# Three of eight second feed-forward products by seven half-size products, and another search for the order

## The chip, the core and the metric

The kernel runs on one core of a Trainium2 chip. The metric is the device time of one execution in microseconds; a kernel's time is the median of its executions. TensorE multiplies, VectorE (DVE) and ScalarE (ACT) work element by element, GpSimd (POOL) does little here, and SyncE (SP) issues the DMAs that bring weights from HBM.

## What is computed

Two layers act on 512 rows of 1024 numbers. Each mixes the rows (a pooling mixer and a sparse attention, from one input projection) and then runs a feed-forward. All is in float32:

```python
for l in range(DEPTH):                       # DEPTH = 2, D_FF = 4096
    h = rms_norm(x, g_pre_mix[l])
    proj = h @ w_in[l]
    ...
    mix = jnp.concatenate([a_out, b_out], axis=-1) @ w_out[l]
    x = x + rms_norm(mix, g_post_mix[l])
    h = rms_norm(x, g_pre_ffn[l])
    f = jnp.square(jax.nn.relu(h @ w_ff1[l])) @ w_ff2[l]
    x = x + rms_norm(f, g_post_ffn[l])
```

The change lies in the line of `f`.

## The kernel before

**Precision.** A float32 number is held as a high half and a low half (value minus high half), both in a format that TensorE takes at full rate. A product is three matmuls (`PASSES`, L823: high by high, high by low, low by high). So every operand of TensorE costs one copy (high half; VectorE or ScalarE, whichever the planner picks, `copy`, L656) and one subtraction (low half; VectorE alone, `tt`, L648).

**Weights.** `WeightStream` (L418) takes all weights in one fixed sequence. Raw tiles come by DMA: two tiles `wraw` for plain loads, two tiles `uraw` (ring `t8`) for units. Each chunk of 128 rows by 512 columns is split into one of eight tiles `ws` (`NWS`, L36), and the next is split when TensorE has used one up (`done`, L581). A unit (`add_unit`, L461) is the weights of one product by sevens: two raw tiles, from which `_combine` (L539) makes fourteen tiles: seven combinations of quarters, each in two parts. Four sums per raw tile (all VectorE) are made in place at the combination S2; a raw tile is given back after its last combination, 22.

**The feed-forward** (L1107 to L1245). The 4096 hidden units are eight blocks of 512. Block 0's first product is plain. For blocks 1 to 7 `unit_products` (L1132) computes the first product of a block as seven products of half size (Winograd's form of Strassen's scheme): 168 matmuls of 256 columns. Three partial results are kept (`kept`), the four quarters are added up, passed through relu and square, and split into `f` (`evac`). Two blocks make a group (`g`, L1184): after both first products comes the group's second product, plain: for each half of the 1024 columns, eight chunks by four row tiles by three passes, into four banks. These are then copied to (first group) or added to (`facc`, VectorE) the sum of the layer, 8 instructions of 512 columns per group.

**Banks.** Eight PSUM banks: a ring of four (`pg`: second product and `unit_products`), a ring of two (`pm`: transposes), two single ones (`pq`). The feed-forward uses the last four only in block 0.

**The order.** The program does not run as written: `Planner` (L83) records each operation with its dependences, the engines it may run on and a cost, and `issue` (L193) searches for an order. A sweep schedules all operations by a key, a second one backward gives each its latest time, and that becomes the next key. `SWEEPS` (L98) is 40, from one beginning; the order with the shortest planned span is issued, each engine's instructions in that order. TensorE's instructions of neighbouring products are mixed where the plan says so. All instructions carry line 372, where the recorder calls the engine, so the rows are read by tiles.

Of the kernel before, what the change touches and what calls it, by code (L numbers as in the profile page):

```python
# [16 lines left out]
OP = mybir.AluOpType  # L17
# [18 lines left out]
NWS = 8  # L36
NRAW = 2
# [45 lines left out]
class Planner:  # L83
# [9 lines left out]
    DMA_LANDS = 1050  # L93
    CELL = 64
# [3 lines left out]
    SWEEPS = 40  # L98
# [89 lines left out]
    def lag(self, ea, eb):  # L188
        if eb == "sp":
            return self.DMA_STARTS  # L190
        return self.DMA_LANDS if ea == "sp" else self.LATENCY.get((ea, eb), 150)

    def issue(self):  # L193

        ops = self.ops
        n = len(ops)
        succ = [[] for _ in range(n)]
        pred = [[] for _ in range(n)]  # L200
        for i, (_, deps, soft) in enumerate(ops):
            for group, hard in ((deps, True), (soft, False)):
                for d in group:
# [9 lines left out]
        state, key, late, best = self.SEED, [], None, None  # L213
        for r in rank:
            state = (state * 1103515245 + 12345) % 2 ** 31
            key.append(self.NOISE * (state / 2.0 ** 31 - 0.5) - r)
        for _ in range(self.SWEEPS):
            start, end, way = self.sweep(key, pred, succ, late)
            span = max(end)
            if best is None or span < best[0]:  # L220
                best = (span, start, way)
            back, _, _ = self.sweep([-t for t in end], succ, pred, None, way)
            late = [span - b for b in back]
            key = [late[i] - ops[i][0][way[i]][1] for i in range(n)]
        self.planned, start, way = best
        for i in sorted(range(n), key=lambda i: (start[i], i)):
            ops[i][0][way[i]][2]()
# [131 lines left out]
class _Recorder:  # L359
# [3 lines left out]
    def __getattr__(self, method):  # L363
        def call(*args, **kw):
# [4 lines left out]
            reads = [a for k, a in list(enumerate(args))[1:] + list(kw.items())  # L369
# [19 lines left out]
    def cost(self, method, args, kw, out, reads):  # L389
# [20 lines left out]
        if self.name == "pool":  # L410
            if method == "memset":
                return 50
            return (70 + 1.2 * n) if method == "tensor_scalar" else (520 if n == 1 else 50 + 2.35 * n)
        nbytes = math.prod(c for _, c in out.ap) * 4
# [3 lines left out]
class WeightStream:  # L418
# [5 lines left out]

    COMBINATIONS = ("11", "12", "S2", "S1", "S3", "S4", "22")

    def __init__(self, copy, tt, sp, raw_pool, ws_pool, unit_pool, sum_pool):
        self.copy, self.tt, self.sp = copy, tt, sp
# [32 lines left out]
    def add_unit(self, src, r0, c0):  # L461

        k = len(self.loads)
        for cp in range(2):
            self.loads.append((src, r0 + 2 * cp * P, "unit", c0, 512))
# [16 lines left out]
    def _ahead(self):  # L482

        while self.n_load < len(self.loads):
            unit = self.loads[self.n_load][2] == "unit"
# [5 lines left out]
    def _load(self):  # L491
# [3 lines left out]
        if n == "unit":  # L495
# [5 lines left out]
            for k in range(2):  # L501
                self.sp.dma_start(t[:, k], src[r + 4 * k * P:r + (4 * k + 2) * P, c0:c0 + ncols].rearrange(
# [36 lines left out]
    def _combine(self, k, name, w):  # L539
# [3 lines left out]

        def quarter(i, j):
            return raw[:, j, :, 256 * i:256 * i + 256]

        def v(ap):
            return ap.rearrange("p (c n) -> p c n", c=2)
# [3 lines left out]
        def halves(value):  # L552
            self.copy(high, value)
            self.tt(low, value, high.bitcast(F32), OP.subtract)
# [31 lines left out]
def hymba_trunk(ctx: ExitStack, tc: tile.TileContext, x, positions, g_pre_mix, w_in, w_pool,  # L586
# [4 lines left out]
        ("pe", nc.tensor), ("act", nc.scalar), ("dve", nc.vector), ("pool", nc.gpsimd), ("sp", nc.sync))]  # L591
    ctx.enter_context(tc.manual_schedule())
# [72 lines left out]
    ws = WeightStream(copy, tt, sp, rawp, wsp, t8p, sup)  # L665
    plan = []
    for l in range(DEPTH):
# [14 lines left out]
        for g in range(4):  # L682
            for b in (2 * g, 2 * g + 1):
                p["ff1", b] = ws.add_unit(w_ff1[l], 0, 512 * b) if b else ws.add(w_ff1[l], 0, D, 512 * b, 512)
            for hf in range(2):
                p["ff2", g, hf] = ws.add(w_ff2[l], 1024 * g, 1024, 512 * hf, 512)
# [183 lines left out]
    for l in range(DEPTH):  # L870
# [261 lines left out]
        def unit_products(ids, f):  # L1132
# [21 lines left out]
            def evac(rows, cols, value, other=None):  # L1154
                r = t2("fr")[:, :512]
                if other is not None:
                    dve.tensor_tensor(r, value, other, op=OP.add)
                    value = r
                planner.either(lambda: act.activation(r, value, AF.Relu),
                               lambda: dve.tensor_scalar(r, value, 0.0, None, op0=OP.max))  # L1160
                squared(r, r)
                rv = r.rearrange("p (j n) -> p j n", j=2)
                hi = f[0][:, 2 * rows:2 * rows + 2, cols]
                copy(hi, rv)
                tt(f[1][:, 2 * rows:2 * rows + 2, cols], rv, hi.bitcast(F32), OP.subtract)
# [4 lines left out]
            evac(0, LATER, two, p1)  # L1170
# [6 lines left out]
            evac(1, SOONER, one, p5)  # L1177
            product(two, "S4", "22")
            evac(0, SOONER, two, u2)
            product(one, "22", "T4")  # L1180
            evac(1, LATER, one)

        facc = None
        for g in range(4):  # L1184
            f1 = []
            for bi in range(2):
                blk = 2 * g + bi
                if bi == 0:
                    f = [c2a.tile([P, 4, S], F32R, name="f1h", tag="c2a"), c2b.tile([P, 4, S], F32R, name="f1l", tag="c2b")]
                else:  # L1190
                    f = c1p.tile([P, 2, 4, S], F32R, name="f1", tag="c1")
                    f = [f[:, 0], f[:, 1]]
                f1.append(f)
                ids = p["ff1", blk]

                def evac_f(j, ps, cols):
                    r = t2("fr")[:, :ps.shape[1]]
                    planner.either(lambda: act.activation(r, ps, AF.Relu),
                                   lambda: dve.tensor_scalar(r, ps, 0.0, None, op0=OP.max))
                    squared(r, r)  # L1200
                    copy(f[0][:, j, cols], r)
                    tt(f[1][:, j, cols], r, f[0][:, j, cols].bitcast(F32), OP.subtract)

                if blk == 0:
                    for tp in (1, 0):
                        cols = slice(256 * tp, 256 * tp + 256)
                        for j in range(4):
                            bank = pq(j, "pf")[:, :256]
                            for kc in range(KC):
                                w = ws.get(ids[kc])  # L1210
                                mm3(bank, lambda a: w[:, a, j * P:(j + 1) * P],
                                    lambda b: A[:, b, kc, cols], kc == 0, kc == KC - 1)
                                if tp == 0 and j == 3:
                                    ws.done()
                            evac_f(j, bank, cols)
                else:
                    unit_products(ids, f)
            if facc is None:
                facc = c0p.tile([P, NT, D], F32, name="facc", tag="c0")
            for hf in range(2):  # L1220
                ids = p["ff2", g, hf]
                cs = slice(512 * hf, 512 * hf + 512)
                banks = [pg() for _ in range(NT)]
                last = g == 3 and hf == 1

                def step(c, t):
                    w = ws.get(ids[c])
                    f = f1[c // 4]
                    mm3(banks[t], lambda a: f[a][:, c % 4, tok(t)], lambda b: w[:, b, :512], c == 0, c == KC - 1)

                for c in range(4 if last else KC):
                    for t in range(NT):
                        step(c, t)
                    ws.done()
                if last:
                    for t in range(NT):
                        for c in range(4, KC):
                            step(c, t)
                            if t == NT - 1:
                                ws.done()  # L1240
                for t in range(NT):
                    if g == 0:
                        copy(facc[:, t, cs], banks[t])
                    else:
                        dve.tensor_tensor(facc[:, t, cs], banks[t], facc[:, t, cs], op=OP.add)  # L1245
        ws.units_allowed = False
# [31 lines left out]
```

## Time and profile before

| | |
|---|---|
| median of three executions | 1188.26 us (1187.7 to 1189.58) |
| the profiled execution | 1189.19 us, span 1187.4 us |
| TensorE busy | 1154.9 us, 97% |
| VectorE busy | 962.8 us, 81% |
| ScalarE busy | 593.5 us, 50% |
| DMA | 115.55 MB, mean 97 GB/s |
| matmuls | 6888 |

The table is of one execution, from its first instruction to its last. Busy time is the time in which at least one instruction of the engine runs; matmuls are pipelined, so a busy TensorE is not yet one at its peak, and its pace has to be read from starts. A stage is judged by itself, since the feed-forward and the attention have different limits.

### The profile page before, as it was taken

What the parts mean: (1) busy time and instruction counts of PE and PEld (TensorE: products, weight loads), DVE (VectorE), ACT (ScalarE), POOL (GpSimd) and SP (SyncE); (2) the same over time, 40 slices, a digit from 0 to 9 for tenths busy, and PEclk for the clock granted to TensorE, in tenths of its full rate; (3) what the DMA queues carried; (4) which work ended last, traced back from release to release, by engine and by line L of the source; (5) the groups of instructions that cost most, each with busy time, mean ns of one, the idle gap of its engine ahead of it and who ended that gap; (6) DMA issues with size and microseconds to landing.
All of it is one profiled execution on the core that took longest, in us unless ns stands there. A gap on an engine that the chain in (4) does not pass through costs nothing.

```text
span 1187.4 us, 18436 instructions
## 1 busy us (share of the span) xinstructions
PE 1154.9 (97%) x6888; PEld 1008.9 (85%) x6888; DVE 962.8 (81%) x2134; ACT 593.5 (50%) x1279; POOL 31.5 (3%) x79
## 2 busy tenths in 40 slices
PE   6999999999999999999999999899999999999997
PEld 6988888789899898899898888777998998988985
DVE  7799999889569579577698999998994785875965
ACT  7545796687226036035275277876760440430621
POOL 2000000010000000000010000001000000000001
PEclk9999998999999999999999999999999999999999
DMA  7221222451423223223233121134542241251231
GB/s 249 71 72 36 71 72 72 142 184 66 161 74 132 95 72 132 82 71 97 60 112 89 54 72 54 54 115 134 160 141 73 71 161 54 72 177 36 72 107 71
DMA packets 62169, 115.55 MB, mean 97 GB/s; under 512 B 5248, under 2 KB 10368, under 8 KB 62080
## 3 DMA queue, kind: packets, MB, share of 16 engines
q1 hardware_dynamic: 62080, 114.38, 30.2%
q8 instruction: 54, 0.88, 0.3%
q14 instruction: 35, 0.29, 0.1%
HBM read 112.27 MB, written 2.10 MB: 96 GB/s over the span
## 4 chain that ended last, share of the span: by engine, by line
PE 61%; DVE 26%; DMA 5%; ACT 4%; issue 3%; POOL 1%; SPq 0%; DVEq 0%; ACTq 0%; POOLq 0%
PE pg L372 33%; PE one L372 9%; PE two L372 7%; DVE ws L372 6%; DVE bias L372 3%; PE pi L372 3%; PE pf L372 3%; DVE m L372 3%; DMA wraw<-in_w_out_dram 2%; DMA uraw<-in_w_ff_dram 2%; DVE mx L372 1%; PE lg L372 1%; DVE s L372 1%; PE po L372 1%; DVE pT L372 1%
## 5 line engine op out<-in xcount | busy, mean ns | idle before, releaser
L372 PE MATMUL pg<-ws,f 128*128 128x512 f32 x768 | 230.5, 394 | 0.0
L372 PE MATMUL pg<-ws,A 128*128 128x512 f32 x864 | 227.5, 401 | 0.9 <-DVE A L372 0.6
L372 ACT ACTIVATE ws<-wraw 128x512 fp32r<-128x512 f32 (+1 forms) x182 | 112.9, 632 | 183.8 <-PE pg L372 127.3
L372 DVE TENSOR_TENSOR ws<-wraw,ws 128x512 fp32r<-128x512 f32 (+1 forms) x288 | 194.4, 689 | 5.9 <-ACT ws L372 3.8
L372 PEld LDWEIGHTS pg<-ws,A 128*128 128x128 f32 x864 | 157.7, 188 | 34.3 <-DVE pn L372 1.6
L372 PE MATMUL pg<-ws,f1h 128*128 128x512 f32 x512 | 167.2, 394 | 0.5 <-ACT fr L372 0.5
L372 PEld LDWEIGHTS pg<-ws,f 128*128 128x128 f32 x768 | 141.1, 188 | 29.0
L372 PEld LDWEIGHTS pg<-ws,f1h 128*128 128x128 f32 x512 | 95.6, 188 | 22.3 <-ACT fr L372 1.0
L372 DVE TENSOR_TENSOR ws<-uraw,ws 128x512 fp32r<-128x512 f32 x168 | 111.7, 686 | 2.0 <-ACT ws L372 0.7
L372 DVE CAST ws<-wraw 128x512 fp32r<-128x512 f32 (+1 forms) x106 | 45.0, 426 | 75.2 <-PE pg L372 64.3
L372 PE MATMUL two<-A,ws 128*128 128x256 f32 x672 | 104.9, 281 | 0.0
L372 PE MATMUL pg<-ws,f1l 128*128 128x512 f32 x256 | 95.8, 393 | 0.0
L372 PEld LDWEIGHTS two<-A,ws 128*128 128x128 f32 x672 | 92.3, 188 | 1.9
L372 ACT ACTIVATE ws<-uraw 128x512 fp32r<-128x512 f32 x95 | 57.7, 627 | 67.8 <-PE pg L372 29.7
L372 ACT ACTIVATE s<-s,st 128x384 f32<-128x384 f32 (+3 forms) x118 | 64.7, 565 | 21.4 <-DVE st L372 20.8
L372 ACT ACTIVATE fr<-fr 128x512 f32<-128x512 f32 (+1 forms) x109 | 63.5, 596 | 21.0 <-DVE fr L372 20.1
L372 DVE TENSOR_TENSOR facc<-pg,facc 128x512 f32<-128x512 f32 x48 | 32.7, 688 | 46.2 <-PE pg L372 46.2
L372 DVE CAST ws<-uraw 128x512 fp32r<-128x512 f32 x73 | 30.4, 424 | 41.7 <-PE pg L372 32.6
L372 PE MATMUL pi<-ws,A 128*128 128x292 f32 x384 | 61.8, 310 | 1.1 <-DVE ws L372 0.8
L372 PE MATMUL pool<-A,ws 128*128 128x512 f32 x192 | 59.2, 405 | 0.0
L372 PEld LDWEIGHTS pg<-ws,f1l 128*128 128x128 f32 x256 | 48.0, 188 | 10.9
L372 PE MATMUL one<-A,ws 128*128 128x256 f32 x336 | 57.0, 280 | 0.0
(189 smaller groups left out, 2203.5 us busy)
## 6 DMA issues: line engine op xcount, KB each, us to landing
wraw<-in_w_ff_dram SPq DMA_DIRECT2D x72, 512.0 KB, 3.8
uraw<-in_w_ff_dram SPq DMA_DIRECT2D x56, 512.0 KB, 4.9
wraw<-in_w_out_dram SPq DMA_DIRECT2D x32, 512.0 KB, 3.7
wraw<-in_w_in_dram SPq DMA_DIRECT2D x24, 512.0 KB, 3.6
wraw<-in_w_in_dram SPq DMA_DIRECT2D x8, 584.0 KB, 4.3
wraw<-in_w_in_dram SPq DMA_DIRECT2D x16, 256.0 KB, 2.9
x<-in_x_dram SPq DMA_DIRECT2D x4, 512.0 KB, 6.5
out_dram<-x SPq DMA_DIRECT2D x8, 256.0 KB, 2.1
```

The lines of the kernel that those rows point to most:

```text
L372: lambda: getattr(self.real, method)(*args, **kw), self.port(method, out, reads))
```

## The change

In blocks 1, 3 and 5 of each layer the second product too is made of seven half-size products; blocks 0, 2, 4, 6 and 7 keep the plain one (`PLAIN_FF2`). The product is now made block by block, not group by group, and block b's second product stands after the first product of block b + 1. The hidden values of a block whose second product goes by sevens are split into seven operands (three quarters and four combinations, with four subtractions) instead of four quarters. The seven products go into two pairs of banks from `pm` and `pq`, and what stands in a pair after each product is added to `facc`, 14 adds per block. The loads of two gains move from the start of the feed-forward to block 6, since the hidden values use their buffers. The search starts from twelve beginnings with 16 sweeps each; all but the first start near the best order so far. A path that would let DMAs do the subtractions is in the code, with nothing selected (`SUMMED_BY_DMA` is empty).

```diff
+PLAIN_FF2 = (0, 2, 4, 6, 7)
...
-    SWEEPS = 40
+    SWEEPS = 16
+    BEGINNINGS = 12
...
+        for begin in range(self.BEGINNINGS):
+            key, late = [], None
+            for i in range(n):
+                state = (state * 1103515245 + 12345) % 2 ** 31
+                mine = -rank[i] if begin == 0 else best[1][i] + best[3][i]
+                key.append(self.NOISE * (1 + 3 * (begin > 0)) * (state / 2.0 ** 31 - 0.5) + mine)
+            for _ in range(self.SWEEPS):
...
+    SUMMED_BY_DMA = {"unit": (), "wide": ()}
...
+    def add_unit(self, src, r0, c0, wide=False):
...
+            if wide:
+                self.loads.append((src, r0 + cp * P, "wide", c0, 1024))
...
+        ff1(0)
+        ff2(0)
+        ff1(1)
+        for b in range(1, 8):
+            if b < 7:
+                ff1(b + 1)
+            ff2(b)
...
-        load_gain(("post_ffn", l), g_post_ffn, l)
-        if l + 1 < DEPTH:
-            load_gain(("pre_mix", l + 1), g_pre_mix, l + 1)
...
+                unit_products(p["ff1", b], put, room)
+                U["T1"] = place(3)
+                U["T2"] = [A[:, a, 0:2, SOONER] for a in range(2)]
+                U["T3"] = [A[:, a, 2:4, SOONER] for a in range(2)]
+                tt(r["11"], r["12"], r["11"], OP.subtract)
+                split(U["T1"], r["11"])
+                tt(r["12"], r["22"], r["12"], OP.subtract)
+                tt(r["22"], r["22"], r["11"], OP.subtract)
+                tt(r["21"], r["21"], r["22"], OP.subtract)
...
+        def ff2_unit(b, U):
+            ids = p["ff2", b]
+            def product(banks, name, other, new, *quarter):
+                for c in range(2):
+                    w = ws.get(ids[name][c])
+                    for t in range(2):
+                        for i, (a, b) in enumerate(PASSES):
+                            pe.matmul(banks[t], U[other][a][:, c, P * t:P * t + P], w[:, b, :512],
+                                      start=new and c == i == 0, stop=c == 1 and i == 2, skip_group_check=True)
+                    ws.done()
+                cs = slice(512 * quarter[0], 512 * quarter[0] + 512)
+                for t in range(2):
+                    acc = facc[:, (2, 0)[quarter[1]] + t, cs]
+                    dve.tensor_tensor(acc, banks[t], acc, op=OP.add)
+            one = [pm("one2"), pm("one2")]
+            two = [pq(i, "two2") for i in range(2)]
+            product(one, "11", "11", True, 0, 0)
+            product(two, "12", "21", True, 0, 0)
+            product(one, "S2", "T2", False, 0, 1)
+            two = [pq(i, "two2") for i in range(2)]
+            product(two, "S1", "T1", True, 1, 1)
+            product(one, "S3", "T3", False, 1, 1)
+            product(two, "S4", "22", False, 0, 1)
+            product(one, "22", "T4", False, 1, 0)
+        f = {0: ff1_block(0)}
+        ff2_plain(0, f.pop(0))
+        f[1] = ff1_block(1)
+        for b in range(1, 8):
+            if b < 7:
+                f[b + 1] = ff1_block(b + 1)
+            if b == 6:
+                load_gain(("post_ffn", l), g_post_ffn, l)
+                if l + 1 < DEPTH:
+                    load_gain(("pre_mix", l + 1), g_pre_mix, l + 1)
+            if b in PLAIN_FF2:
+                ff2_plain(b, f.pop(b))
+            else:
+                ff2_unit(b, f.pop(b))
```

## Rows read from the trace of the kernel before

**Rows 1.** The page's head: span, busy time and share of each engine.
```profile
span 1187.4 us, 18436 instructions
PE 1154.9 (97%) x6888; PEld 1008.9 (85%) x6888; DVE 962.8 (81%) x2134; ACT 593.5 (50%) x1279; POOL 31.5 (3%) x79
```

**Rows 2.** Table by stretch, feed-forward groups: length, busy (instructions), clock, DMA, GB/s.
```profile
core 0: us, PE busy (x) PEld busy (x) DVE busy (x) ACT busy (x) POOL busy (x), PEclk, DMA share, GB/s
381.55:470.55 89.00, 87.69 (x541) 77.96 (x541) 64.32 (x112) 29.44 (x53) 0.00 (x0) 1.00 0.32 106
470.55:552.67 82.12, 81.61 (x516) 73.55 (x517) 59.37 (x104) 27.89 (x48) 0.11 (x1) 1.00 0.25 81
297.17:552.67 255.50, 253.27 (x1583) 226.92 (x1583) 182.72 (x318) 89.09 (x155) 0.11 (x1) 1.00 0.30 100
880.57:1134.47 253.90, 253.37 (x1584) 227.35 (x1584) 182.00 (x319) 85.31 (x149) 0.00 (x0) 1.00 0.30 98
```

**Rows 3.** Chain of waits, in order of time, 280 to 340 us: start, us, what.
```profile
291.03 2.85 PE two L372 x24
293.88 2.70 PE one L372 x23
...
297.17 37.12 PE pg L372 x160
```

**Rows 4.** The page's groups of instructions: the second product's matmuls.
```profile
L372 PE MATMUL pg<-ws,f 128*128 128x512 f32 x768 | 230.5, 394 | 0.0
...
L372 PE MATMUL pg<-ws,f1h 128*128 128x512 f32 x512 | 167.2, 394 | 0.5 <-ACT fr L372 0.5
...
L372 PE MATMUL pg<-ws,f1l 128*128 128x512 f32 x256 | 95.8, 393 | 0.0
```

**Rows 5.** VectorE's longest wait in 276:582 and in 858:1172: total, times, longest.
```profile
DVE ws L372 <- PE pg L372: 50.5, 30, 5.3
DVE ws L372 <- PE pg L372: 46.4, 31, 4.9
```

**Rows 6.** Table by stretch again, columns as in rows 2: around the groups.
```profile
0.00:256.00 256.00, 242.50 (x1341) 205.11 (x1342) 232.70 (x644) 173.80 (x411) 14.26 (x50) 0.98 0.33 101
256.00:276.00 20.00, 18.80 (x155) 18.21 (x156) 17.75 (x30) 14.84 (x34) 0.86 (x1) 1.00 0.55 186
276.00:297.00 21.00, 21.00 (x178) 20.91 (x177) 21.00 (x35) 15.50 (x30) 0.00 (x0) 1.00 0.17 55
...
582.00:830.00 248.00, 242.25 (x1339) 203.07 (x1338) 232.91 (x628) 160.37 (x385) 9.89 (x19) 0.99 0.27 84
830.00:858.00 28.00, 27.15 (x210) 25.18 (x209) 26.89 (x51) 22.79 (x55) 3.04 (x5) 1.00 0.53 170
```

**Rows 7.** Timelines of VectorE and ScalarE: sequences without a gap: start, us, what.
```profile
436.24 1.89 DVE L372 TENSOR_TENSOR ws<-uraw,ws 128x512 fp32r<-128x512 f32 x3
438.05 0.69 DVE L372 TENSOR_TENSOR f1l<-fr,f1h 128x512 fp32r<-128x512 f32 x1
948.17 0.75 DVE L372 CAST ws<-usum 128x512 fp32r<-128x512 f32 x2
445.09 1.15 ACT L372 ACTIVATE ws<-uraw 128x512 fp32r<-128x512 f32 x2 [1.19 <-DMA uraw<-in_w_ff_dram]
```

**Rows 8.** VectorE's groups with casts, 297.2 to 552.7 us: count, busy, mean ns, idle before.
```profile
L372 DVE CAST ws<-uraw 128x512 fp32r<-128x512 f32 x35 | 14.7, 424 | 23.6 <-PE pg L372 17.3 <-PE two L372 3.4 <-DMA uraw<-in_w_ff_dram 1.6
...
L372 DVE CAST ws<-wraw 128x512 fp32r<-128x512 f32 x25 | 10.6, 426 | 24.0 <-PE pg L372 22.9 <-DMA wraw<-in_w_ff_dram 1.0
...
L372 DVE CAST f<-fr 128x512 fp32r<-128x512 f32 x7 | 3.0, 425 | 2.0 <-ACT fr L372 2.0
L372 DVE CAST ws<-usum 128x512 fp32r<-128x512 f32 x6 | 2.5, 422 | 0.2
```

**Rows 9.** Tiles uraw and gain: issues on SP's queue (ns), time to landing (us).
```profile
L372 SPq DMA_DIRECT2D uraw<-in_w_ff_dram x56: 367/414/1332, 257.4 to 1107.0; - x56
...
DMA to landing us min/median/max: 3.6/4.9/7.9
L372 SPq DMA_DIRECT2D gain<-in_g_post_ffn_dram x2: 340/340/340, 256.0 to 841.5; - x2
...
DMA to landing us min/median/max: 3.7/4.9/5.5
```

**Rows 10.** Timeline of VectorE at a seam between two units; in brackets the idle time.
```profile
439.78 0.43 DVE L372 CAST ws<-uraw 128x512 fp32r<-128x512 f32 x1 [1.04 <-DMA uraw<-in_w_ff_dram]
440.24 0.69 DVE L372 TENSOR_TENSOR ws<-uraw,ws 128x512 fp32r<-128x512 f32 x1
440.85 0.68 DVE L372 TENSOR_TENSOR fr<-one,p 128x512 f32<-128x512 f32 x1
442.38 0.69 DVE L372 TENSOR_TENSOR usum<-uraw 128x512 f32<-128x512 f32 x1 [0.85 <-DMA uraw<-in_w_ff_dram]
```

More of the change, by code (lines that the diff above doesn't have):

```diff
@@ L93 @@
     DMA_LANDS = 1050
+    SUM_LANDS = 4900
     CELL = 64
@@ L212, in issue @@
             rank[i] = cost + tail
[L213 to L225, printed above, removed]
+        state, best = self.SEED, None
+        for begin in range(self.BEGINNINGS):
[5 more added lines that the diff above has]
+            for _ in range(self.SWEEPS):
+                start, end, way = self.sweep(key, pred, succ, late)
+                span = max(end)
+                back, _, _ = self.sweep([-t for t in end], succ, pred, None, way)
+                late = [span - b for b in back]
+                key = [late[i] - ops[i][0][way[i]][1] for i in range(n)]
+                if best is None or span < best[0]:
+                    best = (span, start, way, [0.5 * (k - t) for k, t in zip(key, start)])
+        self.planned, start, way, _ = best
         for i in sorted(range(n), key=lambda i: (start[i], i)):
@@ L368, in call @@
                 writes.append(args[7])
-            reads = [a for k, a in list(enumerate(args))[1:] + list(kw.items())
+            reads = ([out] if kw.get("accum_op") is not None else []) + [a for k, a in list(enumerate(args))[1:] + list(kw.items())
                      if isinstance(a, bass.AP) and k not in ("out", "accum_out") and all(a is not w for w in writes)]
@@ L484, in _ahead @@
         while self.n_load < len(self.loads):
-            unit = self.loads[self.n_load][2] == "unit"
+            unit = isinstance(self.loads[self.n_load][2], str)
             kind = "unit" if unit else "raw"
@@ L494, in _load @@
         src, r, n, c0, ncols = self.loads[self.n_load]
-        if n == "unit":
+        if isinstance(n, str):
             self.in_use["unit"] += 1
@@ L553, in halves @@
             self.copy(high, value)
-            self.tt(low, value, high.bitcast(F32), OP.subtract)
+            if name in self.SUMMED_BY_DMA["wide" if wide else "unit"]:
+                self.act.activation(low, high.bitcast(F32), AF.Copy, scale=-1.0)
+                self.gq.dma_start(low, value, accum_op=OP.add)
+            else:
+                self.tt(low, value, high.bitcast(F32), OP.subtract)
         if name in ("11", "12"):
@@ L681, in hymba_trunk, with ff1, ff2 @@
             p["out", pair] = ids
[L682 to L686, printed above, removed]
+        def ff1(b):
+            p["ff1", b] = ws.add_unit(w_ff1[l], 0, 512 * b) if b else ws.add(w_ff1[l], 0, D, 0, 512)
+        def ff2(b):
+            if b in PLAIN_FF2:
+                p["ff2", b] = [ws.add(w_ff2[l], 512 * b, 512, 512 * hf, 512) for hf in range(2)]
+            else:
+                p["ff2", b] = ws.add_unit(w_ff2[l], 512 * b, 0, True)
+        ff1(0)
[5 more added lines that the diff above has]
+            ff2(b)
         plan.append(p)
@@ L1130, in hymba_trunk, with split, relu_squared, unit_products @@
         ws.units_allowed = True
-        def unit_products(ids, f):
+        def split(parts, value):
+            copy(parts[0], value)
+            tt(parts[1], value, parts[0].bitcast(F32), OP.subtract)
+        def relu_squared(r, value, other=None):
+            if other is not None:
+                dve.tensor_tensor(r, value, other, op=OP.add)
+                value = r
+            planner.either(lambda: act.activation(r, value, AF.Relu),
+                           lambda: dve.tensor_scalar(r, value, 0.0, None, op0=OP.max))
+            squared(r, r)
+        def unit_products(ids, put, room):
             one, two = pg("one"), pg("two")
@@ L1152, in kept, with evac @@
                 return k
[L1154 to L1165, printed above, removed]
+            def evac(q, value, other=None):
+                r = room(q)
+                relu_squared(r, value, other)
+                put(q, r.rearrange("p (c n) -> p c n", c=2))
             product(one, "11", "11", True)
@@ L1176, in unit_products @@
             product(one, "S3", "T3")
-            evac(1, SOONER, one, p5)
+            evac("22", one, p5)
             product(two, "S4", "22")
-            evac(0, SOONER, two, u2)
+            evac("12", two, u2)
             product(one, "22", "T4")
-            evac(1, LATER, one)
+            evac("21", one)
         facc = None
[L1184 to L1219, printed above, removed]
@@ L1220, in hymba_trunk, with ff2_plain @@
+        def ff2_plain(b, f):
             for hf in range(2):
-                ids = p["ff2", g, hf]
+                ids = p["ff2", b][hf]
                 cs = slice(512 * hf, 512 * hf + 512)
                 banks = [pg() for _ in range(NT)]
-                last = g == 3 and hf == 1
                 def step(c, t):
                     w = ws.get(ids[c])
-                    f = f1[c // 4]
-                    mm3(banks[t], lambda a: f[a][:, c % 4, tok(t)], lambda b: w[:, b, :512], c == 0, c == KC - 1)
@@ L1231, in hymba_trunk @@
-                for c in range(4 if last else KC):
+                    mm3(banks[t], lambda a: f[a][:, c, tok(t)], lambda b: w[:, b, :512], c == 0, c == 3)
+                if b == 7 and hf == 1:
                     for t in range(NT):
[L1233 to L1237, printed above, removed]
+                        for c in range(4):
                             step(c, t)
@@ L1240, in hymba_trunk @@
                                 ws.done()
+                else:
+                    for c in range(4):
+                        for t in range(NT):
+                            step(c, t)
+                        ws.done()
                 for t in range(NT):
-                    if g == 0:
+                    if b == 0:
                         copy(facc[:, t, cs], banks[t])
```

78 lines of the change are left out of this document (70 added, 8 removed).

## The prediction

> **What bounds the kernel now.** I read the head of the page first: TensorE is busy 97% of the span, VectorE 81%, ScalarE 50%, DMA a third [rows 1]. A busy TensorE need not be one at its peak, so I went to the stage that the change touches, the feed-forward, and cut it into its groups (two blocks of 512 hidden units each: two first products by sevens, then the plain second product). Three groups of each layer lie whole in the trace: 255.50 and 253.90 us for 1583 and 1584 matmuls, 84.9 us per group, at a granted clock of 1.00, the level of 2.4 GHz [rows 2]. In the chain of waits 160 second-product matmuls of 512 columns take 37.12 us, 0.232 each; 24 and 23 of 256 columns take 2.85 and 2.70 us, 0.118 each [rows 3]. A group has 336 of the small and 192 of the large ones (1536 large ones in eight groups [rows 4]): 336 x 0.118 + 192 x 0.232 = 39.6 + 44.5 = 84.2 us. So **TensorE sets the pace here**, with 0.7 us lost per group. VectorE is busy 182.7 and 182.0 us of the three groups, 60.8 per group, and much of its idle time is a wait for TensorE to give a weight tile back: 50.5 and 46.4 us in the two layers' feed-forward [rows 5]. It is idle for lack of space, not of work. Outside the feed-forward it is the other way: VectorE 232.70 of 256 and 232.91 of 248 us [rows 6]; the change removes nothing there.
>
> **What VectorE instructions really cost.** One of 512 columns lasts 0.68 to 0.69 us, but three in a row take 1.89 us, so one more costs (1.89 - 0.69) / 2 = 0.60; two casts take 0.75, one more 0.32; two ScalarE copies 1.15, one more 0.54 [rows 7]. I count by these starts. The Trainium skill ("VectorE: DVE Perf Modes", section "The DRAIN you can't avoid") says that the next operation does not start until the pipe has emptied, though it allows that one which is not held starts earlier; by the strict reading each would cost its whole duration. The rows just named show that these do not.
>
> **The change, part by part.**
>
> *Removed on TensorE.* A plain second product of one block is 96 large matmuls; seven half-size products are 7 x 2 x 2 x 3 = 84. 12 x 0.232 = 2.78 us for each of blocks 1, 3 and 5 in two layers: **-16.7 us**. All of it is on the path as long as TensorE sets the pace.
>
> *Added on VectorE, per such block.* Weights: 14 low halves instead of 8, and 2 x 4 sums: +14. Hidden values: 7 low halves instead of 4, and 4 differences: +7. Sums into the result: the two blocks of a group now add separately, one with 8 adds and one with 14, where 8 stood: +14. That is 35 x 0.60 = 21.0 us for each of six blocks. Group 6, 7 gets 8 more adds, 4.8 us, per layer; the first group's saving differs only in that its first eight are copies. Over both layers: 226 instructions, 136 us. Copies, which may go to either engine: 9 more per block (6 weights, 3 hidden).
>
> *Does that fit?* Per group TensorE now needs 84.2 - 2.8 = 81.4 us. VectorE's 60.8 plus 21.0 is 81.8, if it keeps all its casts. But 73 casts of the three groups are its own (35, 25, 7 and 6), 24 per group and 10 us busy [rows 8], and ScalarE, busy 29 us of 85 [rows 2], can take them at 0.54 each. Without them VectorE needs about 71 of 81. On average it fits; in places it doesn't. A first product by sevens needs 22 instructions for weights and 7 to evacuate (36 in all, where its hidden values are split for seven products), a second one 22 + 14 = 36, each beside 19.8 or 84 x 0.232 = 19.5 us of TensorE; a plain second product 16 beside 22.3. The weight stream is put in the order of use, so a layer has a run of four (ff1 1, ff1 2, ff2 1, ff1 3), two runs of three, and plain blocks between. First run: 36 + 29 + 36 + 36 = 137 x 0.60 = 82.2 us against 78.9; second: 101, 60.6 against 59.1; third: 94, 56.4 against 59.1. The eight weight tiles let VectorE be 8 x 22 / 14 = 12.6 instructions ahead when a run begins, 7.5 us, which covers both excesses (3.3 and 1.5). The stretch 276 to 297 us is the nearest row: VectorE busy 21.00 of 21.00 and TensorE too [rows 6]. So full load alone does not stall it.
>
> *Seams.* A unit's raw tiles are given back only with the last of its combinations, and the next unit's tiles take 4.9 us from issue to landing (3.6 to 7.9) [rows 9]. Between two units VectorE runs dry: 1.04 and 0.85 us at one seam [rows 10]. Today a layer has three such seams, one per whole group; the 0.7 us lost per group is the price at today's load. The change makes it 3 + 2 + 2 = 7: eight more in all. Bounds: nothing (the wait is filled with the additional adds; a seam can't give time back) to 8 x 1.9 = 15 us. By 0.7 they are 5.6; with VectorE fuller I take **+7**, nearer to the row of lost time than to the idle time.
>
> *Banks.* The second product by sevens uses the four banks outside the ring of four, and each of its last five products goes into a pair that was just read by two adds. The wait stands on TensorE, with all its later matmuls behind it. Cover: the product on the other pair, 12 x 0.232 = 2.8 us, against two adds, 0.69 + 0.60 = 1.3. I take 0; without that cover 30 x 1.3 = 39 us, a case that would need VectorE some 1.5 us behind, and so belongs to the rival below.
>
> *Moved.* The loads of the two gains go from the start of the feed-forward to block 6, on SP's queue, past some 20 weight loads. An issue takes 0.34 us and lands within 5.5 [rows 9]; 44 us of plain products follow before the gain is read: 0. The gain buffers now hold hidden values; if a gain waits at SP's head for one, the weight loads behind it wait too, at most the 5.5 us once a layer. The plain second product of block 0 now stands between the first product and the first unit, at a place where VectorE was busy 17.75 of 20 and 26.89 of 28 us and TensorE 18.80 and 27.15 [rows 6]: 0 to 2 us back, I take **-1**. The end of a layer keeps its form: 12 matmuls per row tile behind the last one.
>
> *Longer search.* 12 beginnings of 16 sweeps instead of 40 sweeps: no instruction, but every engine's order is drawn anew. The trace cannot price it. The nearest rows are the same group in different places: 82.12 us with 516 matmuls, 89.00 with 541 [rows 2], the latter some 2 us above the mean of 84.9 once 13 matmuls are allowed for. With eight groups and four other stages I bound it by -8 and +6 and take **-2**.
>
> Sum: -16.7 + 7 - 1 - 2 = -12.7. The profiled execution took 1189.19 us (span 1187.4), 0.9 above the median of 1188.26. Against the median: **1176 us** (1175.6).
>
> **Rivals.**
> (a) *All of it hidden:* seams filled with the new adds, a better order: -16.7 - 1 - 2, 1168. For it: waits of VectorE for space, 97 us over both layers. Against: four units in a row have no precedent here.
> (b) *VectorE takes TensorE's place,* in the runs of units: the other sign. It does if the casts stay on it: 48 on the six units of three groups (35, 6, 7) [rows 8], 8 per unit, 2.6 us. Then the runs need 82.2 + 10.4, 60.6 + 7.8 and 56.4 + 7.8 us, with 1.9 at each of seven seams: 98.3, 72.2, 68.0 against 78.9, 59.1, 59.1, less 7.5 each: 18.9 us per layer late, 37.8 in all, +21 against before. It decides from 8.4 us per layer, when fewer than two in five of these 26 us of casts move. With a quarter moved: 12.4 x 2 - 16.7 = +8, **1196**. For it: ScalarE's copies run late when VectorE's sums come late. Against: ScalarE has 55 us free per group.
> (c) *Seams and full load eat the gain:* 15 us at the new seams, 1187, no change.
> (d) *VectorE pays its whole durations:* runs of 137, 101 and 94 x 0.686 = 94.0, 69.3 and 64.5 us, less 8.6 each, are late by 6.5, 1.6 and 0, 16 us in both layers: 1188. This is the strict reading of the Trainium skill's section named above. Against it stands every sequence of [rows 7].
>
> **How the numbers follow.** The forecast (1170 to 1182) has 0.48; (a) 0.13; between forecast and no change (1182 to 1186) 0.05; (c) 0.11; (d) 0.03; (b) 0.20. A measurement here tells about 0.2%, 2.4 us, from no change: faster 0.48 + 0.13 + 0.05 = 0.66, within 0.14, slower 0.20. The range runs from 1165, (a) with some gain of the search outside the feed-forward, to 1193, which leaves out the upper half of (b).
>
> **What would show it.** 6816 matmuls instead of 6888. Per group, TensorE's time 81 to 83 us; VectorE busy by about 14 to 20 us per group more, ScalarE by 5 to 18; most weight casts on ScalarE. Right: few stalls of TensorE other than at seams, and VectorE's wait for weight space down from 97 us to a fraction. Wrong: TensorE waiting for weight halves (DVE ws) or hidden values over 8 us per layer in the chain of waits, banks of the second product waiting for adds, or another length of the stages outside the feed-forward than 256 and 248 us by over 5 us, which would be the search and not the products.

## The result and the profile after

The changed kernel takes **1176.42 us** (1176.05 to 1178.56) against 1188.74 for the kernel before, a ratio of 0.990 with a 95% interval of 0.9883 to 0.9918. The forecast was 1176, faster. The profiled execution took 1176.31 us, its span 1174.1: 13.3 us less than the span before.

The page's head, which answers to [rows 1], and its chain of waits; the last two lines are the chain of the kernel before:

```profile
span 1174.1 us, 18588 instructions
PE 1137.1 (97%) x6816; PEld 987.6 (84%) x6816; DVE 1068.0 (91%) x2313; ACT 654.8 (56%) x1380; POOL 29.9 (3%) x79
...
PE 50%; DVE 37%; DMA 7%; issue 3%; ACT 2%; POOL 0%; SPq 0%; DVEq 0%; ACTq 0%; POOLq 0%
PE pg L380 20%; PE one L380 12%; DVE ws L380 10%; PE two L380 8%; DVE bias L380 5%; DMA uraw<-in_w_ff_dram 4%; DVE m L380 4%; PE pi L380 3%; DVE s L380 2%; PE pf L380 2%; DVE facc L380 2%; DMA wraw<-in_w_ff_dram 2%; DVE pT L380 2%; DVE uraw L380 2%; DVE mx L380 2%
...
PE 61%; DVE 26%; DMA 5%; ACT 4%; issue 3%; POOL 1%; SPq 0%; DVEq 0%; ACTq 0%; POOLq 0%
PE pg L372 33%; PE one L372 9%; PE two L372 7%; DVE ws L372 6%; DVE bias L372 3%; PE pi L372 3%; PE pf L372 3%; DVE m L372 3%; DMA wraw<-in_w_out_dram 2%; DMA uraw<-in_w_ff_dram 2%; DVE mx L372 1%; PE lg L372 1%; DVE s L372 1%; PE po L372 1%; DVE pT L372 1%
```

There are 72 matmuls fewer, as the products say. TensorE's share is the same, VectorE's rose from 81 to 91%, and in the chain VectorE went from 26 to 37%. To see where the time went, both traces are cut at the same events: a layer's **feed-forward** from the first matmul of its first product (`pf`) to the start of the last one of its second product, and the **mixing** stage (attention) between. First the kernel before, then the changed one, two feed-forwards and two mixing stages each, columns as in [rows 2]:

```profile
248.40:597.70 349.30, 344.69 (x2161) 308.52 (x2160) 259.01 (x449) 137.94 (x264) 6.34 (x8) 1.00 0.31 101
834.20:1178.50 344.30, 343.41 (x2152) 307.92 (x2151) 250.24 (x437) 131.02 (x247) 3.35 (x5) 1.00 0.30 98
9.90:248.40 238.50, 234.27 (x1286) 197.72 (x1286) 220.38 (x620) 163.36 (x389) 8.18 (x15) 0.98 0.31 95
597.90:834.20 236.30, 230.07 (x1286) 192.97 (x1285) 222.68 (x610) 155.02 (x371) 8.99 (x17) 0.99 0.28 86
```

```profile
248.10:588.30 340.20, 338.23 (x2127) 301.68 (x2126) 308.65 (x538) 168.82 (x313) 4.37 (x7) 1.00 0.32 104
823.80:1164.90 341.10, 338.51 (x2118) 300.50 (x2117) 303.12 (x523) 161.29 (x300) 3.88 (x5) 1.00 0.29 98
9.90:248.10 238.20, 229.31 (x1282) 190.88 (x1282) 223.76 (x628) 160.68 (x380) 7.58 (x15) 1.00 0.31 94
588.50:823.80 235.30, 228.58 (x1283) 192.71 (x1282) 221.82 (x605) 157.27 (x377) 9.52 (x17) 0.99 0.29 86
```

The feed-forwards went from 693.6 to 681.3 us, -12.3; the mixing stages from 474.8 to 473.5, -1.3. Against the 16.7 us of matmuls taken out, that leaves 4.4 us of new lost time in the feed-forward. VectorE is busy 102.5 us more there. Its wait for a weight tile to come free, 97 us in [rows 5], is down to 19, in nearly the same stretches (276 to 582 and 858 to 1160 us):

```profile
DVE ws L380 <- PE pg L380: 8.7, 8, 1.6
...
DVE ws L380 <- PE pg L380: 10.4, 8, 2.7
```

The order was drawn anew, so one pair of kernels cannot say what the products did and what the draw did. That is the first experiment.

### The profile page after: what moved, and what is told of

Same layout as the page of the kernel before. It is cut to its first block, busy times and chain, and to the rows that moved or that the text cites. A ratio compares the mean times of both kernels' runs of the same rounds, so it can differ in the third digit from the quotient of the medians.

```text
span 1174.1 us, 18588 instructions
## 1 busy us (share of the span) xinstructions
PE 1137.1 (97%) x6816; PEld 987.6 (84%) x6816; DVE 1068.0 (91%) x2313; ACT 654.8 (56%) x1380; POOL 29.9 (3%) x79
## 4 chain that ended last, share of the span: by engine, by line
PE 50%; DVE 37%; DMA 7%; issue 3%; ACT 2%; POOL 0%; SPq 0%; DVEq 0%; ACTq 0%; POOLq 0%
PE pg L380 20%; PE one L380 12%; DVE ws L380 10%; PE two L380 8%; DVE bias L380 5%; DMA uraw<-in_w_ff_dram 4%; DVE m L380 4%; PE pi L380 3%; DVE s L380 2%; PE pf L380 2%; DVE facc L380 2%; DMA wraw<-in_w_ff_dram 2%; DVE pT L380 2%; DVE uraw L380 2%; DVE mx L380 2%
## 5 line engine op out<-in xcount | busy, mean ns | idle before, releaser
L380 ACT ACTIVATE ws<-uraw 128x512 fp32r<-128x512 f32 x160 | 98.2, 628 | 133.7 <-DMA uraw<-in_w_ff_dram 39.7
L380 DVE TENSOR_TENSOR ws<-wraw,ws 128x512 fp32r<-128x512 f32 (+1 forms) x240 | 161.6, 690 | 3.1 <-ACT ws L380 2.2
L380 DVE TENSOR_TENSOR ws<-uraw,ws 128x512 fp32r<-128x512 f32 x240 | 159.2, 687 | 3.5 <-ACT ws L380 2.6
L380 PE MATMUL two<-A,ws 128*128 128x256 f32 x672 | 116.5, 281 | 0.0
L380 PE MATMUL two<-ws,f 128*128 128x512 f32 x216 | 63.9, 395 | 0.0
L380 DVE TENSOR_TENSOR facc<-pg,facc 128x512 f32<-128x512 f32 x64 | 42.8, 685 | 20.3 <-PE pg L380 20.2
L380 PEld LDWEIGHTS pi<-ws,A 128*128 128x128 f32 x384 | 53.6, 190 | 5.1 <-DVE A L380 1.8
L380 PEld LDWEIGHTS one<-A,ws 128*128 128x128 f32 x336 | 49.4, 188 | 7.2 <-DVE ws L380 1.8
L380 DVE TENSOR_TENSOR uraw<-uraw 128x512 f32<-128x512 f32 x80 | 54.2, 686 | 0.2
L380 PE MATMUL pf<-A,ws 128*128 128x256 f32 x384 | 50.5, 285 | 0.8 <-DVE A L380 0.7
```

The source lines that it names most:

```text
L380: lambda: getattr(self.real, method)(*args, **kw), self.port(method, out, reads))
```

## Experiments

Every run was timed beside the kernel before on the same chip; that stood at 1187.4 to 1188.7 us, on three chips. Lengths of stages are of one profiled execution of each, which can lie some us off the median (1184.83 against 1182.07 for the kernel before with the long search).

### The search and the draw

Two kernels, two searches (short: one beginning of 40 sweeps; long: 12 of 16), two seeds. The changed kernel with the short search (the third with seed 91 too):

```diff
-    SWEEPS = 16
-    BEGINNINGS = 12
+    SWEEPS = 40
+    BEGINNINGS = 1
```

> The changed kernel with the old search (one beginning, 40 sweeps). Theory A (TensorE sets the pace and the 72 matmuls taken out are the gain; the search gives about 2 us): 1176 to 1181 us. Rival S (the longer search made half of the gain or more): 1182 us or more. Theory A expects nearly the whole difference inside the feed-forward.

> The changed kernel with the short search (one beginning, 40 sweeps) and seed 91. If the long search is worth about 3 us: 1173 to 1177 us. If it is worth nothing on this kernel: within 1.5 us of 1171.4; if 6 us, as it was on the kernel before: 1177 us or more.

The changed kernel with the long search and another seed (`SEED = 91` for 53):

> The changed kernel with another seed of the search (91 instead of 53): how much the draw of the order alone moves the time. Theory A: within 3 us of 1176.4. Rival S (a lucky order): 1181 us or more.

The kernel before with the loop of the long search in `issue`, `SWEEPS = 16`, `BEGINNINGS = 12`, with seeds 53 and 91, and with its short search and seed 91:

> The kernel before with the new search (12 beginnings, 16 sweeps each) and nothing else changed. Theory A: 1184 to 1189 us, since the search has only the lost time of the slow group and of the attention to win. Rival S: 1182 us or less.

> The kernel before with the long search and seed 91. If the long search is worth about 3 us whatever the kernel: 1180 to 1185 us, and 9 to 12 us above the changed kernel with the same search and seed (1171.4). If the sevens are worth only the 5.6 us that stand between the two kernels with the long search and seed 53: 1175 to 1178 us.

> The kernel before with its own short search and seed 91. With the next two runs it completes a table of two kernels by two searches by two seeds. If the draw of the order moves every kernel by some 5 us either way: 1182 to 1194 us. If seed 53 was an unlucky draw for the kernel before: 1183 us or less.

| kernel, search, seed | median us | both feed-forwards | both mixing stages |
|---|---|---|---|
| before, short, 53 | 1188.74 | 693.6 | 474.8 |
| before, short, 91 | 1186.38 | 693.2 | 472.0 |
| before, long, 53 | 1182.07 | 694.3 | 470.0 |
| before, long, 91 | 1187.78 | 696.1 | 471.2 |
| changed, short, 53 | 1177.37 | 685.7 | 471.3 |
| changed, short, 91 | 1187.10 | 690.4 | 473.8 |
| changed, long, 53 (the change) | 1176.42 | 681.3 | 473.5 |
| changed, long, 91 | 1171.43 | 680.7 | 468.1 |

Ratios to the kernel before: 0.9907 (0.9892 to 0.9922) for changed, short, 53; 0.9946 (0.9933 to 0.9959) for before, long, 53; 0.9861 (0.9844 to 0.9877) for changed, long, 91; 0.9987 (0.9977 to 0.9996) for changed, short, 91 and for before, short, 91; 0.9995 (0.9986 to 1.0004) for before, long, 91.

Expectations failed both ways. Search and seed together move the changed kernel by up to 15.7 us, more than the whole gain, where my bounds for the search, -8 and +6, were 14 apart. Theory A missed in the kernel before with the long search, 1182.07 where it expected 1184 or more, and with the other seed, 1171.43 where it expected 3 us around 1176.4; rival S missed both times on the changed kernel, 1177.37 and 1171.43. With the short search the time of theory A came true (1176 to 1181), but only 7.9 us of the difference lie in the feed-forward, where it expected nearly all. With seed 91 the long search gave the kernel before nothing (1187.78, above both ranges), and with the short search the changed kernel has no gain (1187.10 against 1186.38). Taken pair by pair, same search and same seed, the changed kernel differs by -11.4, +0.7, -5.7 and -16.4 us. By means of four draws the sevens give 1178.1 against 1186.2, -8.2; the long search gives -2.6 on the kernel before and -8.3 on the changed one, two draws each, too few to tell the two apart.

The stages say more than the medians. The mixing stages, in which the change touches nothing, range from 468 to 475 over the two kernels: the draw, and what one execution differs from another. The feed-forward of the kernel before hardly depends on the draw (693.2 to 696.1), that of the changed one does (680.7 to 690.4). The two sets do not overlap, and the mean falls by 9.8, from 694.3 to 684.5: of 16.7 us of matmuls, 6.9 are lost again. The worst draw, changed, short, 91, spends VectorE's weight halves and the unit loads on the chain, 13 and 6% against the 10 and 4% above, with its feed-forwards at 347.50 and 343.00 us:

```profile
PE pg L380 20%; DVE ws L380 13%; PE one L380 7%; DMA uraw<-in_w_ff_dram 6%; PE two L380 5%; DVE bias L380 4%; PE pi L380 3%; DVE uraw L380 3%; DVE facc L380 3%; DVE m L380 3%; PE pf L380 2%; PE pool L380 2%; PE lg L380 1%; PE po L380 1%; DVE A L380 1%
...
247.70:595.20 347.50, 340.85 (x2125) 300.68 (x2123) 312.58 (x551) 160.76 (x297) 4.87 (x7) 1.00 0.31 101
832.40:1175.40 343.00, 337.79 (x2116) 300.06 (x2115) 304.25 (x529) 157.47 (x292) 5.19 (x5) 1.00 0.29 97
```

### The new arrangement without the sevens

```diff
-PLAIN_FF2 = (0, 2, 4, 6, 7)
+PLAIN_FF2 = (0, 1, 2, 3, 4, 5, 6, 7)
```

> The changed kernel with every second product plain, still block by block and with the new search: 72 matmuls of 512 columns come back (16.7 us of TensorE), of the 113 additional VectorE instructions per layer 32 adds stay. Theory A: 1186 to 1190 us, so that the new arrangement of blocks by itself is worth less than 3 us. Rival S: 1182 us or less. Rival B (VectorE, loaded by the sevens, holds TensorE up, so that they gain less than their matmuls): under 1186, because the stalls go when the sevens go.

1186.65 us, ratio 0.9988 (0.9979 to 0.9997); feed-forwards 697.1, mixing 467.9. That is theory A's range, with a good draw of the mixing stages in it. With the same search and seed the sevens take 15.8 us out of the feed-forward (697.1 to 681.3), nearly their whole 16.7; it is one draw of each. The arrangement by blocks, with 32 more adds per layer, costs the feed-forward 2.8 us against the kernel before with the same search and seed (694.3), or nothing, by the spread of draws; it gives nothing.

### Less and more for VectorE

The low halves of the second products' unit weights as a ScalarE copy; the subtraction is left out, so these weights aren't the right ones. And the same low halves computed twice by VectorE:

```diff
+            elif wide:                                              # the first
+                self.act.activation(low, high.bitcast(F32), AF.Copy, scale=-1.0)
...
             else:
-                self.tt(low, value, high.bitcast(F32), OP.subtract)
+                for _ in range(2 if wide else 1):                   # the second
+                    self.tt(low, value, high.bitcast(F32), OP.subtract)
```

> The changed kernel with the low halves of the second products' weights, where these go by sevens, made by a copy on ScalarE in place of the subtraction on VectorE: 84 VectorE instructions (50 us) less, 84 of ScalarE more; the value minus the high half is left out, so these weights are wrong. Theory A (TensorE's own work is the bound, some 16 us of the feed-forward of both layers are lost): 1168 to 1176 us. Rival B (VectorE is the bound in the runs of units): 1160 us or less.

> The changed kernel with the same low halves computed twice: 84 VectorE instructions (50 us) more, nothing else. It measures how far VectorE is from taking TensorE's place. By the sums of the prediction the first run of a layer has 42 and the others 14 and 14 instructions of slack or less; one unit of the second product carries 14 more. Theory A (slack of some 9% in the feed-forward, in the wrong places): 1184 to 1200 us. Rival B (no slack): 1215 to 1226 us. Ample slack: under 1180 us.

84 instructions less: 1178.24 us, ratio 0.9917 (0.9896 to 0.9938), no gain over the change, and above the ranges of theory A and rival B. 84 more: 1229.57, ratio 1.035 (1.0329 to 1.0372), +53 us for 84 x 0.60 = 50 us of work. Feed-forwards of the first, then of the second:

```profile
244.00:586.00 342.00, 337.19 (x2124) 301.46 (x2123) 300.44 (x534) 168.74 (x313) 6.54 (x7) 1.00 0.31 104
824.30:1167.50 343.20, 338.46 (x2118) 301.44 (x2119) 294.08 (x523) 163.78 (x303) 5.24 (x6) 1.00 0.29 97
```

```profile
247.10:615.10 368.00, 347.38 (x2131) 307.39 (x2130) 332.49 (x572) 172.62 (x321) 3.71 (x7) 0.97 0.29 98
850.20:1221.80 371.60, 347.67 (x2118) 305.69 (x2117) 330.54 (x570) 161.84 (x300) 4.55 (x5) 0.97 0.27 90
```

The first test is weaker than meant: VectorE's busy time fell by only 17 us (611.8 to 594.5), since the search gave it back some 50 casts and copies (188 against 138 in the feed-forwards) and 26 relus (34 against 8 TENSOR_SCALAR). It shows that this much relief, with ScalarE loaded more, buys nothing in this draw. The second contradicts my range (1184 to 1200) and lies above that of rival B: **no slack is to be seen** where the units run, although VectorE is idle for a tenth of the feed-forward. The draws above are at most 15.7 us apart, not 50. In the chain of waits of the second, part of the first run of units is one row of VectorE, here unbroken from 340.04 to 352.64 us, TensorE behind it:

```profile
328.26 4.47 DMA uraw<-in_w_ff_dram
332.75 0.64 ACT ws L380
...
340.04 2.23 DVE ws L380 x4
342.27 1.20 DVE facc L380 x2
343.47 0.60 DVE uraw L380
344.06 1.21 DVE ws L380 x2
345.27 0.60 DVE uraw L380
345.87 6.02 DVE ws L380 x10
351.89 0.61 DVE facc L380
352.64 0.77 PE two L380
```

So rival (b) is real, and lies at most one step behind the change: another 14 instructions per unit of the second product and VectorE sets the pace.

### The seams

Every raw tile of a unit loaded twice, the second load over the first:

```diff
             for k in range(2):
+                for _ in range(2):        # around both dma_start of a unit
```

> The changed kernel with every raw tile of a unit loaded twice, the second load over the first: each seam between two units is longer by 3 us (the transfers alone) to 10 us. There are seven seams in a layer. If the seams are covered (by the eight weight tiles and by the adds that VectorE has waiting): under 1180 us. If the seams carry the time that TensorE still loses (my term of 7 us): 14 times 1.5 to 5 us, 1197 to 1246 us.

A third raw tile, room from scratch tiles:

```diff
-            if self.in_use[kind] >= (2 if unit else NRAW) or unit and not self.units_allowed:
+            if self.in_use[kind] >= (3 if unit else NRAW) or unit and not self.units_allowed:
...
-    t8p = ring("t8p", 2)
+    t8p = ring("t8p", 3)
...
-    t2p = ring("t2p", 6)
+    t2p = ring("t2p", 4)
```

> The changed kernel with a third raw tile for the units, so that half of a unit's weights can be loaded while the unit before still holds its two; the room comes from the scratch tiles of 576 columns (4 instead of 6), which the attention and the evacuation use too. If the seams carry what TensorE still loses in the feed-forward (7.3 and 8.9 us in the two layers): those fall to 3 to 5 us each, 1166 to 1172 us unless the attention loses by its fewer scratch tiles. If the seams are covered today: no fall of the feed-forward, 1175 us or more.

Loaded twice: 1275.53 us, ratio 1.0735 (1.071 to 1.076), +99 us and more than my upper bound. SP's queue waits 197.9 us for first loads before the second ones, 9.9 for each of the 20 units; half as much as these 198 us reaches the end. That is 7 us for each of the 14 seams, or 5 for each unit if those behind a plain product pay too; this run doesn't tell which. TensorE's granted clock falls in this run, too (last section). In both cases the eight weight tiles cover less of a late load than the 7.5 us that I took them to. SP's waits, and what TensorE (its weight loads) waits for most:

```profile
SPq L380 <- DVE ws L380: 718.0, 110, 27.7
SPq L380 <- DMA uraw<-in_w_ff_dram: 197.9, 75, 7.1
...
PEld one L380 <- DVE ws L380: 42.0, 23, 4.5
```

A third tile: **1169.55 us**, ratio 0.9842 (0.9829 to 0.9856). The mixing stages stay (474.0 against 473.5); the feed-forward is shorter by 7.4, 2.6 in the first layer and 4.8 in the second, so that by the expectation's count 4.7 and 4.1 us are still lost, within its 3 to 5:

```profile
248.90:586.50 337.60, 335.64 (x2124) 301.49 (x2123) 311.62 (x544) 166.07 (x309) 3.73 (x7) 1.00 0.32 105
822.10:1158.40 336.30, 334.45 (x2116) 300.90 (x2115) 304.47 (x530) 159.18 (x297) 2.85 (x5) 1.00 0.30 99
...
PE 56%; DVE 31%; ACT 6%; issue 3%; DMA 3%; POOL 1%; POOLq 0%; DVEq 0%; SPq 0%; ACTq 0%
PE pg L380 19%; PE one L380 16%; PE two L380 12%; DVE ws L380 8%; DVE bias L380 4%; PE pi L380 4%; DVE m L380 3%; DMA wraw<-in_w_ff_dram 2%; DVE A L380 2%; DVE pT L380 1%; DVE s L380 1%; ACT s L380 1%; PE lg L380 1%; DVE facc L380 1%; ACT ws L380 1%
```

673.9 us lies 6.8 below the best of the four draws of the changed kernel, outside of what the draw did there. The unit loads, 4% of the chain after the change, are off the list, and VectorE's weight halves fall from 10 to 8%. Idle time before the operations on the raw tile, ended by its load, is 45.3 us in the changed kernel and 29.2 with three tiles, first and last line; 39.7 of the 45.3 are ScalarE's, before its copies of weights. TensorE's own waits for operations on the raw tile, 5.2 us in the second line, are gone with three tiles:

```profile
  DMA uraw<-in_w_ff_dram: 45.3, 34
...
  PEld one L380: 5.2, 12
...
  DMA uraw<-in_w_ff_dram: 29.2, 15
```

This speaks for the load between two units as the carrier of the loss that the sevens brought: with it eased the feed-forward is 19.7 us below the kernel before, 16.7 of matmuls and 3 more. It is one draw, which also has two scratch tiles fewer; the two-tile kernel's four draws are the measure it stands against. In whole times this version beats the kernel before and the change as drawn; the best draw of the change with two tiles, 1171.43, comes within 1.9 us of it by its mixing stages (468.1).

### Shorter runs of units

```diff
-PLAIN_FF2 = (0, 2, 4, 6, 7)
+PLAIN_FF2 = (0, 1, 3, 5, 7)
...
-            if b == 6:
+            if b == 7:
                 load_gain(("post_ffn", l), g_post_ffn, l)
```

> The second product by sevens in blocks 2, 4 and 6 instead of 1, 3 and 5 (the two gains are loaded one block later): runs of two, three, three and two units instead of four, three and three, six seams a layer instead of seven, the same matmuls and the same VectorE instructions. If the long run and the seams carry what TensorE loses: 1171 to 1175 us. If not: within 2 us of 1176.4. It could be slower by a few us where the last run stands before the last plain product.

1171.92 us, ratio 0.9865 (0.9848 to 0.9883), inside the range for which I had named the long run as the cause. The stages do not bear that out: the feed-forwards take 682.5 us, no less than 681.3; the mixing stages, not touched, 468.8. In this draw one seam less per layer and shorter runs gave nothing to be seen; the gain stands outside the feed-forward.

## Why the prediction was right

1176.42 us lies in the range of 1165 to 1193, close to the forecast.

**Matmuls, -16.7.** Held: 6816 matmuls. TensorE was the bound, as the pitch of [rows 3] said. What is left of the 16.7 us is 15.8 between sevens and plain products with the same search and seed, 12.3 against the kernel before, 9.8 in the mean of four draws; the terms -16.7 and +7 make 9.7. Spread over six groups, the 12.3 us take 84.9 us per group to 82.9, inside the 81 to 83 that were to show it.

**VectorE's instructions and the fit.** VectorE has 179 instructions more and ScalarE 101, together the 226 and the 54 copies of the sum; by balance 47 copies moved from VectorE to ScalarE. VectorE's busy time in the feed-forward rose by 102.5 us, 51 per layer; the forecast of 14 to 20 us per group is 42 to 60 for a layer's three. ScalarE's rose by 10 us per group, forecast 5 to 18. That most casts would move to ScalarE failed: in the stretch of the units VectorE still makes 51 casts for unit weights beside ten units, 5.1 each, where six units had 41 [rows 8], 6.8 each; what moved were mostly the plain chunks' (25 to 6), in 263 us where [rows 8] had 256:

```profile
L380 DVE CAST ws<-uraw 128x512 fp32r<-128x512 f32 x41 | 17.2, 423 | 10.1 <-PE pg L380 3.7 <-DMA uraw<-in_w_ff_dram 2.3 <-PE two L380 2.1
L380 DVE CAST ws<-usum 128x512 fp32r<-128x512 f32 x10 | 4.1, 422 | 1.1 <-PE pg L380 1.1
L380 DVE CAST ws<-wraw 128x512 fp32r<-128x512 f32 x6 | 2.6, 425 | 1.2 <-DMA wraw<-in_w_ff_dram 1.2
```

**A sign of being wrong.** I had named over 8 us per layer of weight halves (DVE ws) in the chain of waits. Read by the chain alone, the sign is there: of the second layer's feed-forward they make 2.0% before (7 us) and 16.8% after (57 us); in the first layer it is 27 and 19 us. First the kernel before, then the changed one:

```profile
by line: PE pg L372 49.6%; PE one L372 19.9%; PE two L372 14.7%; PE pf L372 6.5%; DVE ws L372 2.0%; DMA uraw<-in_w_ff_dram 1.4%; DVE x L372 0.8%; DVE facc L372 0.8%; ACT ws L372 0.7%; ACT fr L372 0.6%; DVE uraw L372 0.5%; DVE A L372 0.4%; P
...
by line: PE pg L380 24.1%; DVE ws L380 16.8%; PE one L380 13.6%; PE two L380 9.4%; DMA uraw<-in_w_ff_dram 9.2%; DVE uraw L380 4.3%; DVE facc L380 4.0%; PE pf L380 3.2%; DMA wraw<-in_w_ff_dram 3.1%; DVE r L380 1.6%; issue 1.6%; ACT ws L380 1
```

TensorE itself hardly stood still for them: its weight loads waited some 2 us per layer for VectorE's weight halves, and it was busy 338.5 of these 341.1 us. The chain names what released each step, not what TensorE lost. It shows that the two engines now hand it to and fro, so TensorE alone no longer sets the pace of that stage. The prediction put the two cases under one sign.

**Seams, +7.** The lost time in the feed-forward rose by 4.4 us in this draw and by 6.9 in the mean of four; the third raw tile gives 7.4 back. The term had its size. Its cause rests on the one draw with the third tile; the run with one seam less per layer showed nothing. The sharing out was wrong: I let the lead of eight tiles pay for the runs' excess. By those sums the three runs of a layer had 7, 10 and 17 instructions to spare (7.5 us less 3.3, 1.5 and -2.7, at 0.60; the 42, 14 and 14 of the later expectation do not follow from them), and 14 more in each would have cost 13 us over both layers. The doubled low halves cost 53, so there was no such lead to spend. A seam of the changed kernel, VectorE's timeline; of the two idle times in [rows 10] one is left, the other is filled with other work, adds (`facc`) among it:

```profile
434.98 0.69 DVE L380 TENSOR_TENSOR facc<-one,facc 128x512 f32<-128x512 f32 x1
436.86 0.43 DVE L380 CAST ws<-uraw 128x512 fp32r<-128x512 f32 x1 [1.20 <-DMA uraw<-in_w_ff_dram]
437.21 0.69 DVE L380 TENSOR_TENSOR uraw<-uraw 128x512 f32<-128x512 f32 x1
...
442.36 1.90 DVE L380 TENSOR_TENSOR ws<-uraw,ws 128x512 fp32r<-128x512 f32 x3
```

**Arrangement, -1; search, -2.** Neither was shown. The arrangement gave nothing. The search's term was a guess of the right size for the mixing stages of this draw (-1.3); in the mean of two draws each the long search gave -2.6 and -8.3 us, and single draws of one kernel lie up to 15.7 apart, more than its bounds of -8 and +6. That the forecast met the median within half a microsecond is luck of the draw; the mean of four draws, 1178.1, lies 2 us above it.

**The rivals.** (a) in the feed-forward, 677 us by its sum, was reached only with the third tile (673.9; 1169.55 in all, near its 1168). (b) begins at most 14 instructions per unit further on, but its own condition came true without it: with 5.1 casts per unit of the 8 that it reckoned with, little more than a third moved, fewer than its two in five. By its sum that is 10.7 us per layer late, some 5 us slower in all; measured was 12.3 faster. So the account of the runs charged VectorE too much, and the sign did not hang on the casts as I had it. What was too much (1.9 us at each of seven seams, all work kept inside its run, no plain matmuls among a run's) was not separated; of the last, the first layer shows 28 plain matmuls, some 6.5 us, among those of the units from 292.8 to 379.6 us. (c) happened in one of four draws, 1187.10. (d), whole durations: three subtractions still take 1.90 us in a row, (1.90 - 0.69) / 2 = 0.60 each, under the new load. The strict reading of the Trainium skill ("VectorE: DVE Perf Modes", section "The DRAIN you can't avoid"), that the next operation does not start until the pipe has emptied, stays contradicted for these. Banks: TensorE's weight loads for `one` waited 1.4 us in all for the adds of the layer's result in the second layer; the 0 held. With the doubled low halves, where VectorE was behind, those for `two` waited 9.8, the case that I had left to rival (b).

## What to carry to other kernels

A saving on the bounding engine arrives while the engine that pays for it has slack in the very stretch where it pays, not on the average of the stage: add the work once more in a test kernel and see whether it is free. Where the order of a program is searched for, time each variant with several draws and compare it stage by stage; a stage that the change doesn't touch tells how much of a difference is the draw. And where a stream of loads gives its buffer back only with its last use, one buffer more is worth a run before less work is.

## What the runs showed of the hardware

TensorE's granted clock is 1.00 in the feed-forwards of both kernels, the level of 2.4 GHz. With the doubled low halves, where TensorE waits for VectorE, it is 0.97 in both feed-forwards, and with the doubled loads 0.98 and 0.94: part of the time is spent at the lower level, 1.2 GHz. For the same matmuls TensorE is then busy 695.1 and 713.8 us over both feed-forwards where it was 676.7. How much of the 53 and the 99 us is this clock and how much is waiting was not separated.

Three VectorE subtractions of 512 columns that take 0.69 us each follow one another every 0.60 us, before and after the change.
